# Layer-0 output projection from four plain groups to seven products, with its sums on GpSimd, and all weight sums of the last projection in the z stage

## The chip, the cores and the metric

One core of one Trainium2 chip runs the whole two-layer trunk in one launch. The metric is device time in microseconds (us): the median of three runs of the kernel before is 1525.44 us (1524.47 to 1526.9). Profiles are of one execution on the same core; times in them count from the start of its span. Engines are named as the profile names them: PE (TensorE, matmuls), PEld (its weight loads), DVE (VectorE), ACT (ScalarE), POOL (GpSimd) and SP (the queue that issues the DMAs).

## The reference, cut to what matters

The sequence has 1024 positions, the model 1024 columns, everything is float32. Layer 0 projects its input once, runs a chunked gating unit and a pooling mixer beside each other, gates both, concatenates them to 2048 columns and maps them back; layer 1 is latent attention with a gate and an output projection of the same shape.

```
x <- LN(alpha * x + (1 + gate) * sublayer(x * (1 + scale) + shift))     # both layers
even_mixer: a = gmlp(u, LN(v)) * silu(z_a);  b = pool(x_b) * silu(z_b)
            return concatenate([a, b], -1) @ w_out       # (1024 x 2048) @ (2048 x 1024), layer 0
mla_mixer:  return (o * silu(z)) @ w_out                 # the same shape, layer 1
```

The change concerns the line with `concatenate([a, b]) @ w_out`, and the preparation of layer 1's `w_out`.

## The kernel before, in words

**Numbers in two parts.** A float32 product is made of three fp32r matmuls (`mm3`, L107 to L114): high part times high part, high times low, low times high. `split` (L116 to L121) makes the parts: the high part is a rounding copy on ScalarE (L120), the low part the difference, on VectorE or GpSimd (L121). A tile of 128x1024 (two blocks of 128 rows by 512) is the usual unit; 46 slots of that size (`T`) are shared by all stages, so a load waits until a slot is free.

**Layer 0 in front of the projection.** The input projections run step by step; the u, v, z_a steps are in a seven-product (Strassen-Winograd) form over halves of both operands. The last step is u6 (names u6a to u6d and u6o). Its result is multiplied by the gating unit's output (`gmlp_out`, one half on GpSimd, L829, one on VectorE) and stored to `mix_d` in memory, as are all other blocks of the concatenated activations.

**The output projection of layer 0** (`OutPlain`, object `OP0`) is plain: four groups (two halves of the positions by two halves of the columns), each of 8 chunks q of 256 rows of the contraction, each chunk 4 row tiles x 2 x 3 = 24 matmuls of 128x512 (names y, f0A.., f0W..). Per chunk it loads 512 KB of weights and, in the first and third group, 512 KB of activations, and splits them (ScalarE, VectorE). `evac` applies gate, residual and statistics on VectorE; `norm` and `done0` end a row tile. `to_hT` (names hx, xf, g) turns the rows of the first half for layer 1, in `hook0` at i = 24.

**What the projection carries along** (`hook0`, one call per chunk): the rope tables (`rope_tables`, L1377 to L1400, names ang, kk, RT: some 20 instructions on VectorE of 128x256), three groups of absorbed key weights (`absorb`: each 20 small matmuls, names uk, uq, wab), and two of the four sets of weight sums.

**Weight sums.** The output projection of layer 1 (`OutGated`, object `OP1`) is in the seven-product form. Its weight operands are made ahead: `weight_sums(q)` loads four blocks of `w_out`, multiplies them with the gate on VectorE (L1426), makes four differences on GpSimd (L1431) and stores seven blocks to `wf_d`. Two sets are made in layer 0's projection, two in the z stage.

**The z stage** projects layer 1's gate: eight steps z0 to z7, z0 plain, the others seven products of 12 matmuls each. Every one of these seven steps makes its weight operands with six instructions on GpSimd and five low parts on VectorE, each 128x512, three products ahead of their use. Background work lies in the queue `bg`, from which `pump` takes some after each product.

**What sets the order.** The program is written as one sequence; a scheduler then places the instructions of every engine in a fixed order, in which each engine runs them one after the other, waiting at an instruction until its operands are there. The order of every engine is therefore known, and an instruction that waits holds up all that stand behind it on its engine.

`OutProj`, the parent class of `OutGated`, is in the file before too, and is not used directly: its `prep` takes the engine of each sum and low part from the table `ENG`, by layer and chunk.

Of the kernel before, what the change touches and what calls it, by code (L numbers as in the profile page):

```python
# [17 lines left out]
P = 128  # L18
# [19 lines left out]
ORDER = (1, 6, 5, 7, 4, 3, 2)  # L38


ENG = ({"1B": "VVVV", "1A": "VVVV", "2B": "VVVV", "2A": "GGGG", "6a": "GGGG", "6b": "VVVV",
        "6B": "VVVV", "6c": "VVVG", "6d": "VVGV", "6A": "GGGG", "5B": "VVVV", "5A": "GGGG",
        "7a": "VVVV", "7B": "VVVV", "7b": "VVVV", "7A": "VVVV", "4a": "GGGG", "4B": "VVVV",
        "4A": "VVVV", "3B": "VVVV", "3a": "GGGG", "3A": "VVVV"},
       {"1B": "VVGV", "1A": "VGVG", "2B": "VVVG", "2A": "GGGG", "6a": "GGGG", "6b": "VVVV",
        "6B": "VVVV", "6c": "VVVG", "6d": "VVVV", "6A": "GGGG", "5B": "VVVV", "5A": "GGGG",
        "7a": "VGVG", "7B": "VVVV", "7b": "VVGG", "7A": "GGGG", "4a": "GGVG", "4B": "GVVV",
        "4A": "GGGV", "3B": "VVVV", "3a": "GGGG", "3A": "VVGV"})

NORM = ("MDMDMDDD", "ADADADAD")  # L50

# [29 lines left out]
def trunk_kernel(ctx, tc, x, c, positions, ada_w, ada_b, ln_g, ln_b, e_w_in, gmlp_norm_g,  # L81
# [12 lines left out]
    def T(shape, dt, name):  # L94
        return tp.tile(shape, dt, tag="T", name=name)

    def S2(shape, dt, name):
        return s2.tile(shape, dt, tag="s2", name=name)
# [4 lines left out]
    def B1(shape, name):  # L103
        return pp.tile(shape, F32, tag="b1", name=name)
# [248 lines left out]
    bg = deque()  # L353
# [10 lines left out]
    def mm_nt(HF, W):  # L364

        wf, nkk = W.out, W.nkk

        def mm(ps, fa, fb, start, u):
            for kk in range(4):
                w, h = wf[fa, kk // nkk], HF[fb, kk]  # L370
                mm3(ps, w[:, 0, kk % nkk, :], w[:, 1, kk % nkk, :], h[:, 0, :], h[:, 1, :],
                    start and kk == 0, kk == 3, not start)
        return mm
# [214 lines left out]
    def absorb(g, dma=None):  # L588
        dma = dma or (lambda out, in_: SY.dma_start(out=out, in_=in_))
        uk = S2([P, GH, P], F32, f"uk{g}")  # L590
        uq = [S2([P, GH, NOPE], F32, f"uq{g}{rt}") for rt in range(2)]
        ukT = [None]

        def load():
            dma(out=uk, in_=mla_w_uk[0, :, g * GH:(g + 1) * GH, :])
            for rt in range(2):
                dma(out=uq[rt], in_=mla_w_uq[0, rt * P:(rt + 1) * P, g * GH:(g + 1) * GH, 0:NOPE])

        def turned(src, nm, eng):
            ps = B1([P, GH, P], nm + "p")  # L600
            for h in range(GH):
                PE.transpose(ps[:, h, :], src[:, h, :], ident)
            t = S2([P, GH, P], F32, nm + "T")
            eng(out=t, in_=ps)
            return t

        uqT = [None] * 2

        def keys():
            ukT[0] = turned(uk, f"uk{g}", V.tensor_copy)  # L610

        def query(rt):
            uqT[rt] = turned(uq[rt], f"uq{g}{rt}", A.copy)

        def product(rt):
            wp = B1([P, GH, P], f"wab{g}{rt}")
            for h in range(GH):
                PE.matmul(wp[:, h, :], lhsT=uqT[rt][:, h, :], rhs=ukT[0][:, h, :], start=True, stop=True)
            wab = S2([P, GH * P], F32, f"wabs{g}{rt}")
            V.tensor_scalar(out=wab, in0=wp.rearrange("p h d -> p (h d)"), scalar1=gq[:, rt:rt + 1],  # L620
                            scalar2=None, op0=ALU.mult)
            SY.dma_start(out=wab_d[g, :, rt, :], in_=wab)

        return [load, lambda: (keys(), query(0)), lambda: (product(0), query(1)), lambda: product(1)]
# [12 lines left out]
    n = 0  # L637
# [258 lines left out]
    class OutProj:  # L896
# [45 lines left out]
        def prep(self, p, q):  # L942
# [4 lines left out]
            def eng(x_):  # L947
                return G if ENG[self.l][x_][q] == "G" else V

# [392 lines left out]
    def to_hT(th, Z):  # L1342
        for kk in range(4):
            xt = T([P, 2, 512], F32, f"xf{th}{kk}")
            xf[th, kk] = xt
            for j in range(2):
                k = kk + 4 * j
                ps = B1([P, 512], f"hx{th}{k}")
                for tt in range(4):
                    t = th * 4 + tt  # L1350
                    PE.transpose(ps[:, tt * P:(tt + 1) * P],
                                 Z[k // 4, t // 2][:, t % 2, (k % 4) * P:(k % 4 + 1) * P], ident)
                if XF[th][k] == "A":
                    A.activation(out=xt[:, j, :], in_=ps, func=AF.Identity,
                                 bias=fold[:, 1, k:k + 1], scale=fold[:, 0, k:k + 1])
                else:
                    V.tensor_scalar(out=xt[:, j, :], in0=ps, scalar1=fold[:, 0, k:k + 1],
                                    scalar2=fold[:, 1, k:k + 1], op0=ALU.mult, op1=ALU.add)
                H1.new(form_key(k, th), xt[:, j, :], G if XL[th][k] == "G" else V, f"g{k}_{th}")
# [46 lines left out]
    def weight_sums(q):  # L1406


        r = {}
        IJ = [(i, j) for i in range(2) for j in range(2)]  # L1410

        def load():
            if not gate1:
                g1 = T([P, D], F32, "gate1")
                SY.dma_start(out=g1, in_=gate_d[1].partition_broadcast(P))
                gate1.append(g1)
            for i, j in IJ:
                t = r[i, j] = T([P, 2, 512], F32, f"ws{q}{i}{j}")
                k0 = i * 1024 + q * 256
                SY.dma_start(out=t, in_=o_w_out[0, k0:k0 + 256, j * 512:(j + 1) * 512]  # L1420
                             .rearrange("(k p) c -> p k c", p=P))

        def gated(i, j, n):
            t = r[i, j]
            g1 = gate1[0][:, j * 512:(j + 1) * 512].unsqueeze(1).to_broadcast([P, 2, 512])
            V.tensor_tensor(out=t, in0=t, in1=g1, op=ALU.mult)  # L1426
            if n:
                SY.dma_start(out=wf_d[n - 1, q], in_=t)

        def made(n, to, a, b):  # L1430
            G.tensor_tensor(out=r[to], in0=r[a], in1=r[b], op=ALU.subtract)  # L1431
            SY.dma_start(out=wf_d[n - 1, q], in_=r[to])

        return [load, lambda: None,
                lambda: (gated(0, 0, 1), gated(0, 1, 0)), lambda: (gated(1, 1, 3), gated(1, 0, 2)),
                lambda: made(5, (0, 1), (0, 1), (0, 0)), lambda: made(6, (1, 1), (1, 1), (0, 1)),
                lambda: made(7, (0, 0), (1, 1), (0, 0)), lambda: made(4, (1, 0), (1, 0), (1, 1))]

    later_groups = []
    later_sums = []  # L1440

    def hook0(i):
        if i == 6:
            rope_tables()
        if i % 8 in (1, 2, 3, 4) and i < 24:
            if i % 8 == 1:
                later_groups.extend(absorb(1 + i // 8))
            later_groups.pop(0)()
        if i < 24:
            if i % 12 == 2:  # L1450
                later_sums.extend(weight_sums(i // 12))
            if later_sums:
                later_sums.pop(0)()
        if i == 24:
            to_hT(0, Zs)

    def mix_unit(t, th, q):
        m = 2 * q
        SY.dma_start(out=t, in_=mix_d[m:m + 2, :, th * 512:(th + 1) * 512].rearrange("m d t -> d m t"))

    OP0 = OutPlain(0, e_w_out[0], mix_unit, x[0], done0, (0, 1), (4, 5, 6, 7, 0, 1, 2, 3),
                   lambda n, nm: [B1([P, 512], nm + str(u)) for u in range(4)], hook0)

    def early0(p):
        if p == 1:
            OP0.load_to(0)
        if p in (3, 4):
            OP0.prep_to(p - 3)
        if p == 5:
            OP0.load_to(3)  # L1470
        if p == 6:
            OP0.gate()

# [14 lines left out]
    for s, (stp, post) in enumerate(plan):  # L1488
        nm = stp.nm
# [31 lines left out]

    OP0.run()

# [225 lines left out]

    for m in range(8):  # L1750
        o = [T([P, 2, 512], F32, f"zo{m}{i}") for i in range(2)]
        if m in (1, 4):
            bg += weight_sums(2 + m // 4)
        if m == 0:
            plain(l1, 0, H1, lambda i, j, ps: A.activation(out=o[i][:, j, :], in_=ps, func=AF.Silu))
        else:
            strassen(l1, m, mm_nt(H1, zsteps[m]), lambda u, i, j: o[i][:, j, :], 1, f"z{m}", 3,
                     early1 if m == 7 else None)
        for i in range(2):
            if m:  # L1760
                A.activation(out=o[i], in_=o[i], func=AF.Silu)
            SY.dma_start(out=z_d[2 * m + i], in_=o[i].rearrange("p a b -> p (a b)"))
# [120 lines left out]
    n = len(items)  # L1883
# [36 lines left out]
    for m in range(n):  # L1920
        g, i, first, last = items[m]
# [67 lines left out]
```

## Time and profile before

| | |
|---|---|
| median of three runs | 1525.44 us |
| profiled execution, whole | 1528.2 us |
| its span | 1526.4 us |
| TensorE busy | 1478.0 us, 97% |
| VectorE / ScalarE / GpSimd busy | 69% / 41% / 43% |
| DMA, mean | 138 GB/s |
| granted TensorE clock, mean | 0.99 |

The stages by the trace: input projections of layer 0 until 505 us, its output projection from 505 to some 700, latents of layer 1 (kvq) until 745, z until some 905, attention until 1350, the last projection until the end. A row of the timeline gives start, duration, engine, line, operation, output and inputs (buffer numbers left out, so that tiles of one name read alike), how many instructions it merges, and, in brackets, how long the engine had been idle and what ended that. Durations include a wait that an instruction meets after it has started, so the same instruction can take longer in one place than in another.

### The profile page before, as it was taken

What the parts mean: (1) busy time and instruction counts of PE and PEld (TensorE: products, weight loads), DVE (VectorE), ACT (ScalarE), POOL (GpSimd) and SP (SyncE); (2) the same over time, 40 slices, a digit from 0 to 9 for tenths busy, and PEclk for the clock granted to TensorE, in tenths of its full rate; (3) what the DMA queues carried; (4) which work ended last, traced back from release to release, by engine and by line L of the source; (5) the groups of instructions that cost most, each with busy time, mean ns of one, the idle gap of its engine ahead of it and who ended that gap; (6) DMA issues with size and microseconds to landing.
All of it is one profiled execution on the core that took longest, in us unless ns stands there. A gap on an engine that the chain in (4) does not pass through costs nothing.

```text
span 1526.4 us, 21181 instructions
## 1 busy us (share of the span) xinstructions
PE 1478.0 (97%) x7875; PEld 1269.7 (83%) x7875; DVE 1047.3 (69%) x1660; ACT 622.8 (41%) x1122; POOL 652.0 (43%) x583
## 2 busy tenths in 40 slices
PE   7999998999999999999999999999999999999997
PEld 5888776998898888888888878898989889878885
DVE  6557859574567596556766446777777777668598
ACT  3433323323323323425433445554544545555351
POOL 0033427376567023115776632454444442234245
PEclk9999999999999999999999999999999999999999
DMA  9725543103202799612375551131231131274532
GB/s 300 193 70 200 200 173 110 57 28 111 83 28 90 277 383 333 232 56 77 111 275 193 193 162 59 56 111 42 70 97 56 56 103 33 94 261 139 179 125 97
DMA packets 130771, 210.47 MB, mean 138 GB/s; under 512 B 11774, under 2 KB 78052, under 8 KB 130668
## 3 DMA queue, kind: packets, MB, share of 16 engines
q1 hardware_dynamic: 130668, 209.12, 40.5%
q8 instruction: 62, 1.02, 0.3%
q14 instruction: 41, 0.34, 0.1%
HBM read 152.46 MB, written 56.63 MB: 137 GB/s over the span
## 4 chain that ended last, share of the span: by engine, by line
PE 79%; DVE 9%; DMA 5%; issue 2%; ACT 2%; SPq 1%; POOL 1%; DVEq 0%; POOLq 0%; ACTq 0%
PE pt L1853 4%; PE y L113 3%; PE y L114 3%; PE y L112 3%; PE sc L1785 2%; PE av L113 2%; PE av L112 2%; PE av L114 2%; PE sc L1787 2%; PE sc L1786 2%; PE sc L1789 2%; PE sc L1788 2%; PE zb L113 2%; PE zb L114 2%; DVE mc L753 1%
## 5 line engine op out<-in xcount | busy, mean ns | idle before, releaser
L1836 POOL TENSOR_SCALAR p<-p,rz 128x1024 f32<-128x1024 f32 (+5 forms) x96 | 82.3, 858 | 175.3 <-DVE rz L1835 157.4
L120 ACT CAST pth<-pt 128x512 fp32r<-128x512 f32 x144 | 82.0, 590 | 79.9 <-PE pt L1853 78.9
L121 DVE TENSOR_TENSOR pth<-pt,pth 128x512 fp32r<-128x512 f32 x144 | 96.1, 687 | 24.6 <-ACT pth L120 23.7
L1832 ACT ACTIVATE p<-sc,nm 128x1024 f32<-128x1024 f32 (+5 forms) x96 | 81.8, 853 | 57.4 <-DVE nm L1824 45.9
L1824 DVE TENSOR_REDUCE nm<-sc 128x1 f32<-128x1024 f32 (+5 forms) x96 | 85.1, 887 | 2.0 <-DVE rz L1835 0.2
L1853 PE MATMUL pt<-ident,p 128*128 128x128 f32 x576 | 84.6, 272 | 0.1
L1853 PEld LDWEIGHTS pt<-ident,p 128*128 128x128 f32 x576 | 69.6, 140 | 11.3 <-DVE ol L121 0.3
L1785 PE MATMUL sc<-kvTh,qlh 128*128 128x512 f32 (+4 forms) x192 | 70.6, 368 | 8.3 <-ACT p L1804 3.2
L1431 POOL TENSOR_TENSOR ws<-ws,ws 128x1024 f32<-128x1024 f32 x16 | 43.4, 2724 | 75.0 <-DVE ws L1426 51.8
L1788 PE MATMUL sc<-KRh,qrT 128*128 128x512 f32 (+4 forms) x192 | 66.7, 348 | 0.0
L1789 PE MATMUL sc<-KRl,qrT 128*128 128x512 f32 (+4 forms) x192 | 66.4, 346 | 0.0
L1787 PE MATMUL sc<-kvTh,qll 128*128 128x512 f32 (+4 forms) x192 | 66.3, 345 | 0.0
L1786 PE MATMUL sc<-kvTl,qlh 128*128 128x512 f32 (+4 forms) x192 | 66.1, 344 | 0.0
L112 PE MATMUL av<-pth,kvh 128*128 128x512 f32 x144 | 61.1, 425 | 1.0 <-ACT pth L120 1.0
L113 PE MATMUL av<-pth,kvh 128*128 128x512 f32 x144 | 60.2, 418 | 0.2 <-DVE pth L121 0.2
L114 PE MATMUL av<-pth,kvl 128*128 128x512 f32 x144 | 56.7, 394 | 0.0
L753 DVE SCALAR_TENSOR_TENSOR mc<-mw,cT,mc 128x1024 f32<-128x1024 f32 x28 | 47.5, 1698 | 9.2 <-DMA mw<-in_ada_w_dram 8.8
L1245 POOL TENSOR_TENSOR r1A<-r1A,r1A 128x1024 f32<-128x1024 f32 x12 | 32.3, 2700 | 44.7 <-DMA r1A<-o_d 34.8
L121 DVE TENSOR_TENSOR ol<-av,oh 128x512 fp32r<-128x512 f32 x32 | 22.0, 687 | 39.7 <-ACT oh L120 39.7
L1785 PEld LDWEIGHTS sc<-kvTh,qlh 128*128 128x128 f32 x192 | 36.5, 190 | 14.6 <-ACT p L1832 5.6
L120 ACT CAST oh<-av 128x512 fp32r<-128x512 f32 x32 | 18.8, 587 | 60.1 <-PE av L114 59.7
L1550 POOL TENSOR_TENSOR qrf<-qrf 128x256 f32<-128x256 f32 x32 | 23.6, 737 | 44.6 <-DVE rz L1835 20.1
(1887 smaller groups left out, 5147.8 us busy)
## 6 DMA issues: line engine op xcount, KB each, us to landing
mw<-in_ada_w_dram SPq DMA_DIRECT2D x32, 512.0 KB
r0W<-in_e_w_out_dram SPq DMA_DIRECT2D x32, 512.0 KB
wf_d<-ws SPq DMA_DIRECT2D x28, 512.0 KB
r1W<-wf_d SPq DMA_DIRECT2D x28, 512.0 KB
ada<-in_ada_w_dram SPq DMA_DIRECT2D x32, 256.0 KB
r0A<-mix_d SPq DMA_DIRECT2D x16, 512.0 KB
ws<-in_o_w_out_dram SPq DMA_DIRECT2D x16, 512.0 KB
z_d<-zo SPq DMA_DIRECT2D x16, 512.0 KB
```

The source lines that it names most:

```text
L112: PE.matmul(ps, lhsT=lh, rhs=rh, start=start, stop=False, skip_group_check=more)
L113: PE.matmul(ps, lhsT=lh, rhs=rl, start=False, stop=False, skip_group_check=more)
L114: PE.matmul(ps, lhsT=ll, rhs=rh, start=False, stop=stop, skip_group_check=more)
L120: A.copy(out=hi, in_=src)
L121: eng.tensor_tensor(out=lo, in0=src, in1=f(hi), op=ALU.subtract)
L1785: PE.matmul(o, lhsT=qh[:, h, qs], rhs=kvTh[:, ks], start=True, stop=False)
L1786: PE.matmul(o, lhsT=qh[:, h, qs], rhs=kvTl[:, ks], start=False, stop=False)
L1787: PE.matmul(o, lhsT=qo[:, h, qs], rhs=kvTh[:, ks], start=False, stop=False)
L1788: PE.matmul(o, lhsT=qt[:, h, :], rhs=KRh[:, ks], start=False, stop=False)
L1789: PE.matmul(o, lhsT=qt[:, h, :], rhs=KRl[:, ks], start=False, stop=True)
L1824: V.tensor_reduce(out=nm, in_=sv, axis=AX.XY, op=ALU.max, negate=True)
L1853: PE.transpose(ps[:, h, :], pl[h][:, j * P:(j + 1) * P], ident)
```

## The change

The object `OP0` becomes an `OutProj`: 28 chunks (7 products of 4), 24 matmuls each, in the order of products 1, 6, 5, 7, 4, 3, 2 (names y0a to y0d, f0A.., f0B.., chunk names by place in that order and q, so f0A12 is the activation operand of the second product, 6, in chunk 2). The operands of products 6, 7, 4 and 3 are sums of blocks: for each q four for product 6, two for 7, one each for 4 and 3, all 128x1024. The new table `ENG` puts every sum on GpSimd (keys in small letters) and every low part on VectorE. Halves are taken in the other order: the second half of the positions first, and the pooling branch's half of the contraction as the first block column.

`hook0` now makes the rope tables at chunk 8 (before: 6) and two groups of key weights in the first eight chunks. The last group of key weights, and all four sets of weight sums, move to the z stage (steps 1, 2, 4 and 5).

```diff
-ENG = ({"1B": "VVVV", "1A": "VVVV", "2B": "VVVV", "2A": "GGGG", "6a": "GGGG", "6b": "VVVV",
...
+ENG = ({k: ("GGGG" if k[1].islower() else "VVVV")
+        for k in ("1B", "1A", "2B", "2A", "6a", "6b", "6B", "6c", "6d", "6A", "5B", "5A", "7a", "7B",
+                  "7b", "7A", "4a", "4B", "4A", "3B", "3a", "3A")},)
...
     later_groups = []
-    later_sums = []
 
     def hook0(i):
-        if i == 6:
+        if i == 8:
             rope_tables()
-        if i % 8 in (1, 2, 3, 4) and i < 24:
-            if i % 8 == 1:
-                later_groups.extend(absorb(1 + i // 8))
+        if i < 8:
+            if i % 4 == 0:
+                later_groups.extend(absorb(1 + i // 4))
             later_groups.pop(0)()
-        if i < 24:
-            if i % 12 == 2:
-                later_sums.extend(weight_sums(i // 12))
-            if later_sums:
-                later_sums.pop(0)()
         if i == 24:
             to_hT(0, Zs)
 
-    def mix_unit(t, th, q):
-        m = 2 * q
+    def mix_unit(t, th, kh, q):
+        m = kh * 8 + 2 * q
         SY.dma_start(out=t, in_=mix_d[m:m + 2, :, th * 512:(th + 1) * 512].rearrange("m d t -> d m t"))
 
-    OP0 = OutPlain(0, e_w_out[0], mix_unit, x[0], done0, (0, 1), (4, 5, 6, 7, 0, 1, 2, 3),
-                   lambda n, nm: [B1([P, 512], nm + str(u)) for u in range(4)], hook0)
+    OP0 = OutProj(0, e_w_out[0], mix_unit, x[0], done0, (1, 0), (1, 0),
+                  lambda x_, nm: [B1([P, 512], nm + str(u)) for u in range(4)], hook0)
 
     def early0(p):
         if p == 1:
-            OP0.load_to(0)
+            OP0.load_to(1)
...
-        if m in (1, 4):
-            bg += weight_sums(2 + m // 4)
+        if m == 1:
+            bg += absorb(3)
+        if m in (1, 2, 4, 5):
+            bg += weight_sums(m - 1 - m // 4)
```

What `OutProj.prep` does for a chunk of product n (unchanged code that layer 0 now runs; `sub` runs on the engine that `ENG` names, `op` splits):

```
elif n == 6:
    sub("6a", "B12", "B12", "B11")
    sub("6b", "B22", "B22", "B12")
    op("B", p, q, r["B22", q], eng("6B"))
    sub("6c", "A21", "A21", "A22", ALU.add)
    sub("6d", "A11", "A21", "A11")
    op("A", p, q, r["A11", q], eng("6A"))
elif n == 5:
    ab(r.pop(("B12", q)), r.pop(("A21", q)))
elif n == 7:
    sub("7a", "B11", "B22", "B11")
    op("B", p, q, r.pop(("B11", q)), eng("7B"))
    r["S3", q] = T([P, 2, 512], F32, f"r{self.l}S3{q}")
    sub("7b", "S3", "A22", "A11")
    op("A", p, q, r.pop(("S3", q)), eng("7A"))
elif n == 4:
    sub("4a", "B22", "B21x", "B22")
```

**GpSimd at the start of the projection, before.** After the two products with the gating unit (u4o, u6o) stand the first weight sums (ws, set 0):

```order
L829 TENSOR_TENSOR u4o0_3935<-u4o0_3935,gA4_3725 128x1024
L829 TENSOR_TENSOR u6o0_4137<-u6o0_4137,gA6_3929 128x1024
L1431 TENSOR_TENSOR ws001_4424<-ws001_4424,ws000_4422 128x1024
L1431 TENSOR_TENSOR ws011_4428<-ws011_4428,ws001_4424 128x1024
L1431 TENSOR_TENSOR ws000_4422<-ws011_4428,ws000_4422 128x1024
L1431 TENSOR_TENSOR ws010_4426<-ws010_4426,ws011_4428 128x1024
```

The same place after the change, from u6o on. A name such as r0A210 is the raw block A21 of chunk q = 0:

```order
L824 TENSOR_TENSOR u6o0_4137<-u6o0_4137,gA6_3929 128x1024
L946 TENSOR_TENSOR r0A210_2_4270<-r0A210_2_4270,r0A220_2_4272 128x1024
L946 TENSOR_TENSOR r0B110_0_4173<-r0B220_2_4268,r0B110_0_4173 128x1024
L946 TENSOR_TENSOR r0B121_2_4274<-r0B121_2_4274,r0B111_1_4177 128x1024
L946 TENSOR_TENSOR r0A110_0_4175<-r0A210_2_4270,r0A110_0_4175 128x1024
L946 TENSOR_TENSOR r0A211_2_4278<-r0A211_2_4278,r0A221_2_4280 128x1024
L946 TENSOR_TENSOR r0B122_3_4282<-r0B122_3_4282,r0B112_1_4179 128x1024
L946 TENSOR_TENSOR r0B221_2_4276<-r0B221_2_4276,r0B121_2_4274 128x1024
L946 TENSOR_TENSOR r0A212_3_4286<-r0A212_3_4286,r0A222_3_4288 128x1024
L946 TENSOR_TENSOR r0B123_3_4290<-r0B123_3_4290,r0B113_1_4181 128x1024
L946 TENSOR_TENSOR r0A111_1_4183<-r0A211_2_4278,r0A111_1_4183 128x1024
L946 TENSOR_TENSOR r0B222_3_4284<-r0B222_3_4284,r0B122_3_4282 128x1024
```

Two sums (6a and 6b of chunk 0) stand ahead of u6o; the twelve after it go on with 6c, 7a, 6a, 6d of several chunks in turn. The last sum of product 6 (6d of chunk 3) is the 18th after u6o, and four of 7b follow.

**VectorE in the same stage, before.** The rope table's steps (ang, kk) lie between low parts of the first and second group (f0A07l, f0W10l), eight of them in a row:

```order
L1377 TENSOR_TENSOR ang_4599<-inv_109,C_97 128x256
L1381 TENSOR_SCALAR kk_4601<-ang_4599 128x256
L121 TENSOR_TENSOR f0A07l_4531<-r0A07_4430,f0A07h_4530 128x1024
L1383 TENSOR_SCALAR kk_4601<-kk_4601 128x256
L121 TENSOR_TENSOR f0W07l_4535<-r0W07_4432,f0W07h_4534 128x1024
L1384 TENSOR_SCALAR kk_4601<-kk_4601 128x256
L1385 TENSOR_SCALAR kk_4601<-kk_4601 128x256
L121 TENSOR_TENSOR f0W10l_4571<-r0W10_4481,f0W10h_4570 128x1024
```

After the change they lie between the low parts of product 6 (f0B12l, f0A12l and f0B13l, chunks 2 and 3), with steps of the first product's result (y002, its residual x002):

```order
L1372 TENSOR_TENSOR ang_4741<-inv_109,C_97 128x256
L116 TENSOR_TENSOR f0B12l_4548<-r0B222_3_4284,f0B12h_4547 128x1024
L1376 TENSOR_SCALAR kk_4743<-ang_4741 128x256
L1010 SCALAR_TENSOR_TENSOR y002_4481<-x002_4531,y002_4481 128x512 x2
L1378 TENSOR_SCALAR kk_4743<-kk_4743 128x256
L1379 TENSOR_SCALAR kk_4743<-kk_4743 128x256
L1380 TENSOR_SCALAR kk_4743<-kk_4743 128x256
L1382 TENSOR_TENSOR kk_4743<-kk_4743 128x256
L1385 SCALAR_TENSOR_TENSOR ang_4741<-kk_4743,ang_4741 128x256 x2
L116 TENSOR_TENSOR f0A12l_4554<-r0A112_1_4185,f0A12h_4553 128x1024
L1385 SCALAR_TENSOR_TENSOR ang_4741<-kk_4743,ang_4741 128x256 x2
L116 TENSOR_TENSOR f0B13l_4604<-r0B223_3_4292,f0B13h_4603 128x1024
```

Nine instructions now stand between the two low parts of chunk 2. From z7 on, the orders of all engines are the same before and after, but for a few places.

## Rows read from the trace of the kernel before

**Rows 1.** Page, busy time and share of each engine, whole span

```profile
PE 1478.0 (97%) x7875; PEld 1269.7 (83%) x7875; DVE 1047.3 (69%) x1660; ACT 622.8 (41%) x1122; POOL 652.0 (43%) x583
```

**Rows 2.** Windows: length, PE, PEld, DVE, ACT, POOL busy, PEclk, DMA share, GB/s

```profile
505.00:560.00 55.00, 55.00 (x258) 45.83 (x257) 45.32 (x48) 20.89 (x24) 13.23 (x5) 1.00 0.95 346
560.00:610.00 50.00, 49.58 (x233) 41.13 (x232) 37.94 (x42) 17.39 (x19) 12.82 (x7) 1.00 0.99 344
```

**Rows 3.** Timeline of PE, start of the projection: start, duration, what

```profile
505.61 0.39 PE L112 MATMUL y<-f0W00h,f0A00h 128*128 128x512 f32 x1
...
510.82 0.39 PE L114 MATMUL y<-f0W00h,f0A00l 128*128 128x512 f32 x1
...
531.03 1.05 PE L618 MATMUL wab<-uk1T,uq10T 128*128 128x128 f32 x8
```

**Rows 4.** Timeline of POOL in the projection, 440 to 720 us

```profile
514.74 2.41 POOL L829 TENSOR_TENSOR u6o<-u6o,gA 128x1024 f32<-128x1024 f32 x1 [17.45 <-DVE u6o L406]
...
549.48 7.50 POOL L1431 TENSOR_TENSOR ws<-ws,ws 128x1024 f32<-128x1024 f32 x3 [9.67 <-DVE ang L1390]
...
596.20 2.39 POOL L1431 TENSOR_TENSOR ws<-ws,ws 128x1024 f32<-128x1024 f32 x1 [4.57 <-DMA wf_d<-ws]
...
665.69 5.05 POOL L121 TENSOR_TENSOR g<-xf,g 128x512 fp32r<-128x512 f32 x4 [45.85 <-ACT g L120]
```

**Rows 5.** Timeline of POOL in the last projection, 1372 to 1387 us

```profile
1373.15 12.43 POOL L1245 TENSOR_TENSOR r1A<-r1A,r1A 128x1024 f32<-128x1024 f32 x4 [4.61 <-DVE f1A03l L121]
```

**Rows 6.** Timeline of DVE in the same stretch

```profile
1373.69 2.96 DVE L121 TENSOR_TENSOR f1B10l<-r1W,f1B10h 128x1024 fp32r<-128x1024 f32 x1
1376.57 3.41 DVE L121 TENSOR_TENSOR f1A10l<-r1A,f1A10h 128x1024 fp32r<-128x1024 f32 x1
1379.90 1.28 DVE L1877 TENSOR_TENSOR zt<-uvp,zt 128x512 f32<-128x512 f32 x2
...
1383.26 3.41 DVE L121 TENSOR_TENSOR f1A11l<-r1A,f1A11h 128x1024 fp32r<-128x1024 f32 x1
```

**Rows 7.** Timeline of DVE, 545 to 561 us

```profile
546.61 5.71 DVE L1390 SCALAR_TENSOR_TENSOR ang<-kk,ang 128x256 f32<-128x256 f32 x8
552.35 2.37 DVE L1391 TENSOR_SCALAR ang<-ang 128x256 f32<-128x256 f32 x1
554.76 2.51 DVE L1396 SCALAR_TENSOR_TENSOR kk<-ang 128x256 f32<-128x256 f32 x1
557.19 0.28 DVE L1394 TENSOR_SCALAR RT<-RT 128x256 f32<-128x256 f32 x1
...
557.59 1.21 DVE L121 TENSOR_TENSOR f0W11l<-r0W,f0W11h 128x1024 fp32r<-128x1024 f32 x1
558.73 0.68 DVE L1162 TENSOR_TENSOR y<-y,gate 128x512 f32<-128x512 f32 x1
559.33 0.28 DVE L1400 COPY RT<-RT 128x256 f32<-128x256 f32 x1
```

**Rows 8.** Timeline of PE after its longest wait in layer 0

```profile
260.95 0.79 PE L113 MATMUL pm<-ph,pw 128*128 128x512 f32 x1 [4.25 <-DVE ph L121]
...
262.82 0.63 PE L112 MATMUL za0a<-hT,za0S 128*128 128x512 f32 x1
263.25 0.63 PE L113 MATMUL za0a<-hT,za0S 128*128 128x512 f32 x1
```

**Rows 9.** Windows behind that wait

```profile
261.00:263.00 2.00, 2.00 (x5) 1.61 (x6) 1.66 (x2) 0.83 (x2) 1.16 (x2) 0.50 0.00 0
...
267.00:269.00 2.00, 2.00 (x11) 1.61 (x10) 1.03 (x2) 1.63 (x3) 0.09 (x1) 1.00 0.04 8
```

**Rows 10.** Window of the z stage with its densest set of weight sums

```profile
785.00:805.00 20.00, 20.00 (x89) 16.55 (x90) 14.47 (x13) 8.92 (x16) 17.67 (x11) 1.00 0.75 257
```

**Rows 11.** Page, costliest groups: sums on POOL in the last projection

```profile
L1245 POOL TENSOR_TENSOR r1A<-r1A,r1A 128x1024 f32<-128x1024 f32 x12 | 32.3, 2700 | 44.7 <-DMA r1A<-o_d 34.8
```

**Rows 12.** Groups by line and form: high parts of 128x1024 on ACT

```profile
L120 ACT CAST wz0h<-wz0r 128x1024 fp32r<-128x1024 f32 x2 | 2.1, 1052 | 0.0
```

## What was predicted before the run

> **What bounds the kernel now.** I read the page's busy shares first, then the window table of the layer-0 output projection, then the timelines of TensorE, GpSimd and VectorE around its start. TensorE is busy 97% of the span [rows 1], and in the two windows after 505 us [rows 2] it is busy 55.00 of 55 and 49.58 of 50 us at a granted clock of 1.00: the projection is a stretch in which TensorE never waits, and GpSimd is idle three quarters of it (13.23 and 12.82 us busy). The timeline of TensorE [rows 3] gives the pace: from 505.61 to 510.82 lie 23 steps of one 128x512 matmul, 0.2265 us each. So a matmul taken out is worth 0.2265 us, as long as its successors find their operands. DMA engines are at 0.95 and 0.99 in those windows without TensorE waiting; the change moves fewer bytes there, and I count no gain for it.
>
> **What goes.** The plain form has 4 groups x 8 chunks x 24 = 768 matmuls, the seven-product form 28 x 24 = 672. 96 x 0.2265 = **21.7 us less**. The third group of the absorbed key weights moves to z with its 20 small matmuls; it costs TensorE the same there and is left out of the sum.
>
> **What comes: the sums, and who needs them.** Each of the four chunks q of product 6 needs four sums of 128x1024 on GpSimd (6a, 6b for the weights, 6c, 6d for the activations), then a high part on ScalarE and a low part on VectorE. In the new order of GpSimd the last one, 6d of q=3, stands 18 sums behind the product u6o, because four sums for product 7 (7a) lie between. u6o starts at 514.74 in the trace, when VectorE is done with it [rows 4]; no sum but the first two can go ahead of it.
>
> What a sum costs depends on VectorE. Alone it takes 2.39 us [rows 4]. Where both engines work out of SBUF, they take turns: between 1373.15 and 1385.58 four sums take 12.43 us, and in the same stretch VectorE's low parts of 128x1024, which take 1.21 elsewhere, take up to 3.41 us, while two products that read PSUM take 1.28 together [rows 5, 6]. 3.41 is 2.39 plus one low part at its pace of 1.14 (1.21 at 557.59, the next instruction at 558.73). It holds for small instructions too: of eight 128x256 steps of the rope table in 5.71 us one stands in a sum, the next two take 2.37 and 2.51 where 0.28 is usual, and the three sums beside them take 7.50 us, 2.50 each [rows 4, 7]. So while GpSimd has a sum ready, VectorE gets one instruction per sum, however small, and GpSimd loses that instruction's time.
>
> The Trainium skill (SBUF — State Buffer, section "SBUF: two separate sides") says that the pair of ports VectorE and GpSimd share is an exclusive lock for a whole instruction, taken by whichever starts first, against VectorE instructions in a two-port mode or with two SBUF inputs. The trace agrees that the loser stands still, and it adds that the waiting engine comes next, which the page does not say. Were there no turns, and GpSimd kept the ports until its queue is dry, f0A02l of product 1 would come only 22 x 2.39 = 52.6 us after 518, near 571; six chunks (32.6) and the small matmuls (5.2) follow it, and product 6 would end near 609, 12 us later than by turns. The 12.43 us of [rows 5] speak against that; the dear case below has room for it.
>
> Now the turns, by the new orders of both engines. Low part f0B02l takes the ports first (514.5 to 515.6), u6o follows, and GpSimd is at 518.0.
> - Chunk 0 of product 6 gets its last operand at 535.6: 6 sums (14.3) and A02l, B03l, A03l, B10l, A10l. TensorE is there at 532.6 (96 steps, 12 of u6, 20 small ones) and loses 2 to 3 us at most.
> - Chunk 1 needs f0A11l. From 518.0 there are 12 sums (28.7), seven low parts (8.0) and four 128x512 products with the gate at 0.60 (2.4): 557.1. The copy of the key weights that the next small matmuls need (uk2T) stands behind f0B11l on VectorE, so TensorE already waits before them, from about 541 to 552.
> - Chunk 2 needs f0A12l. The order puts nine instructions of VectorE between f0B12l and f0A12l, seven of them of the rope table, and GpSimd has 10 sums left (the four of 7b are ready and follow at once). 10 x 2.39 = 23.9, plus the turns of VectorE between them (one low part 1.14, two residual steps 1.2, six rope steps 1.6): GpSimd is dry at 584.9; two rope steps and the low part itself: 586.8.
> - Chunk 3 needs f0A13l, 12 more instructions with GpSimd idle: 593.4. Then 16 matmuls: product 6 ends at 597.0.
>
> Without a wait it would end at 505.6 + 192 x 0.2265 (43.5) + 12 matmuls of the last u step (2.7) + 40 small matmuls of two groups of key weights (5.2, at 1.05 for eight, [rows 3]) = 557.0. So the wait costs **40.0 us**. The loads do not set it: the last one for 6c (q=3) is issued behind a store at about 552 and 6c comes at 566.
>
> **After product 6.** Products 5, 7, 4 and 3 have no sum of their own in the way until 4a and 3a, eight sums of 2.39 us. VectorE needs per product eight low parts (9.1) and some eleven 128x512 steps (6.6): 63 of 4 x 21.7 = 87 us, and 19 us in which it stands behind a sum make 82. Nearly full, so a wait of some us is likely where two sums come together: **4 us** (0 to 12; 12 is five of the eight sums uncovered). Product 2 and the start of kvq have the same chain as today.
>
> **Clock.** A wait of 4.25 us at 256.7 was followed by the clock at 0.50 and a pace of 0.43 a matmul (262.82, 263.25) until 266, some twelve, and at 1.00 again in the window from 267 [rows 8, 9]: 12 x 0.20 = 2.4 us. After the long waits of chunk 1 and 2 the same is due; most of it falls into the next wait. **2 us** (0 to 7, three such starts).
>
> **z.** Two more sets of weight sums lie there: 8 sums, 8 products with the gate. The ports again: a z step (84 matmuls, 19.0 us) has six 128x512 instructions on GpSimd at 1.26 (5.05 for four, [rows 4]) and five low parts at 0.60, 10.6 us; a set has 4 x 2.39 + 4 x 1.14 = 14.1. Seven steps hold 133 us; the ports are taken for 102 now and 131 after. Where the set lies densest today, TensorE is busy 20.00 of 20 [rows 10], so the low end is 0. In z2 to z7, where the order puts all 16 sums, 6 x 10.6 + 56.4 = 120 stands against 114 us: 6 over, and twice that if the queues lose as much in waiting. I take **5 us** (0 to 12).
>
> **Sum.** -21.7 + 40.0 + 4 + 2 + 5 = +29.3 us on the span of 1526.4, so 1555.7. The profiled execution took 1528.2 in all, and the median of the runs is 1525.4, 1.0 below the span; the forecast for the median is **1555 us**.
>
> **Rivals.**
> - GpSimd alone is the bound; no turns. For it: the projection of layer 1 runs sums too and its line shows 2.70 us a sum, not 3.4 [rows 11]. Against: that is a mean over covered and bare ones, and [rows 5] shows the turns. 18 sums from 517.15: 560.2 at 2.39, 566.1 at 2.72; high part 1.05 [rows 12], then a chunk: product 6 ends at 566.7 to 572.6, 9.7 to 15.6 late. With 2 us of clock -10.0 to -4.1: 1515 to 1521, faster. The point from which this decides: a wait under 21.7 us, so fewer than about half of VectorE's turns.
> - No wait at all, the sums done in time: 1525.4 - 21.7 = 1504. For it only that GpSimd is idle in the stage; against it that 18 sums at 2.39 are 43 us from 517 and TensorE wants the last at 551.
> - z and the tail come dearer: the ports full from 745 on, 12 in the tail, 7 of clock, 15 to 20 in z: -21.7 + 40.0 + 12 + 7 + 18 = +55, 1580. For it the 131 of 133; against it that a z step's operands are prepared three products ahead, so that a queue may fall behind for a while.
>
> **How the numbers follow.** The turns as above 0.68 (1538 to 1570 by the bounds of its terms), GpSimd alone 0.13, no wait 0.03, dearer 0.16. The range 1528 to 1578 leaves out the two faster cases and part of the dear one. A measurement of this kernel tells 0.2% (3 us) from no change: faster 0.14 (the two cases less their edge), same 0.03, slower 0.83.
>
> **What would show it.** In the changed kernel's timeline: sums on GpSimd in a row from about 518 to 585; low parts f0A10l to f0B12l and the rope steps at 2.4 us and more; TensorE waiting for f0A12l (line of the low part) some 24 us, for uk2T and f0A11l some 12 together, for f0A13l a few; the end of product 6 near 597; 672 matmuls for y0. The forecast is wrong if rope steps between sums take 0.3 us, if the sums take 2.39 each with low parts at 1.2 beside them, or if TensorE has no wait over 10 us before 600.

## The result, and the profile after

The changed kernel takes **1546.94 us** (median of four runs, 1545.01 to 1547.57), the kernel before 1524.95 on the same chip: ratio 1.0148, 95% interval 1.0135 to 1.0161. It is slower by 22 us; the forecast was 1555. The profiled execution took 1547.57 us, its span is 1545.8, 19.4 more than the span before.

The page's busy times of the changed kernel: instructions of each engine behind the x. TensorE has 96 matmuls fewer in all and is busy 11.5 us less, in a span that is longer (its share fell from 97%) [rows 1].

```profile
PE 1466.5 (95%) x7779; PEld 1255.5 (81%) x7779; DVE 1110.9 (72%) x1692; ACT 636.6 (41%) x1142; POOL 759.5 (49%) x615
```

Where the time went is read from the first matmul of each stage. TensorE's timeline of the kernel before, first matmul of kvq, z0 and attention:

```profile
697.41 0.56 PE L112 MATMUL kvq<-wkh,g 128*128 128x448 f32 x2
743.58 0.39 PE L112 MATMUL wz<-g,wz0h 128*128 128x512 f32 x1
900.08 0.28 PE L112 MATMUL qlp<-q0h,wa 128*128 128x256 f32 x1
```

The changed kernel: first matmul of y, of product 5 (where product 6 has ended), kvq, z0 and attention:

```profile
505.93 0.39 PE L107 MATMUL y0a<-f0B00h,f0A00h 128*128 128x512 f32 x1
...
586.11 0.39 PE L107 MATMUL y0c<-f0B20h,f0A20h 128*128 128x512 f32 x1
...
704.96 0.36 PE L107 MATMUL kvq<-wkh,g 128*128 128x448 f32 x1
...
749.25 0.40 PE L107 MATMUL wz<-g,wz0h 128*128 128x512 f32 x1
...
921.21 0.28 PE L107 MATMUL qlp<-q0h,wa 128*128 128x256 f32 x1
```

| stage | before, us | after, us | difference |
|---|---|---|---|
| up to the first y | 505.61 [rows 3] | 505.93 | +0.3 |
| y, to the first kvq | 191.80 | 199.03 | +7.2 |
| kvq | 46.17 | 44.29 | -1.9 |
| z | 156.50 | 171.96 | +15.5 |
| attention and the rest of the span | 626.3 | 624.6 | -1.7 |

So there are two places: the projection, which should have become 24 us shorter and became 7 longer, and z. Each column is one execution, and the stage before y varies by 2 to 3 us even between versions that differ only in z (first y at 505.93 and 503.85, 505.18 and 502.06), so single us mean little here; 7 and 15 do not come from that.

The windows that answer to [rows 2], in the same columns (length, PE, PEld, DVE, ACT and POOL busy, PEclk, DMA share, GB/s):

```profile
505.00:560.00 55.00, 44.47 (x205) 37.07 (x204) 46.81 (x26) 16.89 (x22) 50.64 (x18) 0.88 0.59 211
560.00:610.00 50.00, 40.62 (x168) 32.75 (x167) 45.03 (x47) 19.19 (x23) 27.81 (x8) 0.90 0.17 54
```

TensorE is busy 85 of 105 us where it was busy 104.6; GpSimd went from 13.2 to 50.6 us in the first window. The DMA engines stand at 0.17 in the second, and the long waits below are for VectorE, so the loads don't set the pace. TensorE's timeline at its two long waits (in brackets, idle time before and what ended it):

```profile
550.23 2.05 PE L613 MATMUL wab<-uk2T,uq20T 128*128 128x128 f32 x8 [9.13 <-DVE uk2T L599]
552.07 1.06 PE L597 MATMUL uq21p<-ident,uq 128*128 128x128 f32 x4
553.80 2.08 PE L613 MATMUL wab<-uk2T,uq21T 128*128 128x128 f32 x8 [0.68 <-ACT uq21T L599]
555.53 0.77 PE L107 MATMUL y0a<-f0B11h,f0A11h 128*128 128x512 f32 x1
...
574.46 0.80 PE L109 MATMUL y0a<-f0B12h,f0A12l 128*128 128x512 f32 x1 [9.25 <-DVE f0A12l L116]
575.05 0.63 PE L107 MATMUL y0a<-f0B12h,f0A12h 128*128 128x512 f32 x1
575.47 0.63 PE L108 MATMUL y0a<-f0B12l,f0A12h 128*128 128x512 f32 x1
```

Both are waits for VectorE, and after each the matmuls come at 0.43 us instead of 0.23, at a granted clock of 0.50 (1.2 of 2.4 GHz); at 1.00 the pace is back. Windows in the columns of [rows 2]:

```profile
550.00:554.00 4.00, 3.10 (x13) 2.73 (x14) 0.83 (x2) 0.84 (x2) 4.00 (x3) 0.50 0.02 7
...
574.50:578.50 4.00, 4.00 (x10) 3.17 (x11) 3.93 (x8) 0.00 (x0) 0.00 (x0) 0.50 0.00 0
580.00:584.00 4.00, 4.00 (x19) 3.30 (x18) 3.64 (x4) 0.35 (x1) 0.00 (x0) 1.00 0.21 79
```

GpSimd's timeline, where [rows 4] had one product and a few weight sums:

```profile
515.06 3.31 POOL L824 TENSOR_TENSOR u6o<-u6o,gA 128x1024 f32<-128x1024 f32 x1 [3.12 <-DVE u6o L401]
518.33 3.36 POOL L946 TENSOR_TENSOR r0A<-r0A,r0A 128x1024 f32<-128x1024 f32 x1
521.65 6.68 POOL L946 TENSOR_TENSOR r0B<-r0B,r0B 128x1024 f32<-128x1024 f32 x2
...
553.96 2.37 POOL L946 TENSOR_TENSOR r0A<-r0A,r0A 128x1024 f32<-128x1024 f32 x1
...
565.47 2.39 POOL L946 TENSOR_TENSOR r0B<-r0B,r0B 128x1024 f32<-128x1024 f32 x1
567.82 2.78 POOL L946 TENSOR_TENSOR r0A<-r0A,r0A 128x1024 f32<-128x1024 f32 x1
591.57 14.82 POOL L946 TENSOR_TENSOR r0S<-r0A,r0A 128x1024 f32<-128x1024 f32 x3 [20.97 <-PE y0c L108]
```

Eighteen sums run without a gap from 518.33 to 570.60, 2.90 us each. Then GpSimd stands still for 20.97 us: the four sums 7b (written to the new tiles r0S) start only when matmuls of product 5 have released a slot. VectorE's timeline, from the stretch in front of the first wait on, in the form of [rows 7]:

```profile
535.68 10.52 DVE L1009 TENSOR_TENSOR y<-y,gate 128x512 f32<-128x512 f32 x4
546.12 3.35 DVE L116 TENSOR_TENSOR f0B11l<-r0B,f0B11h 128x1024 fp32r<-128x1024 f32 x1
549.40 0.68 DVE L599 COPY uk2T<-uk2p 128x512 f32<-128x512 f32 x1
...
554.73 2.68 DVE L116 TENSOR_TENSOR f0A11l<-r0A,f0A11h 128x1024 fp32r<-128x1024 f32 x1 [1.66 <-ACT f0A11h L115]
...
558.00 1.93 DVE L1372 TENSOR_TENSOR ang<-inv,C 128x256 f32<-128x256 f32 x1
559.85 3.42 DVE L116 TENSOR_TENSOR f0B12l<-r0B,f0B12h 128x1024 fp32r<-128x1024 f32 x1
563.19 2.47 DVE L1376 TENSOR_SCALAR kk<-ang 128x256 f32<-128x256 f32 x1
565.59 5.57 DVE L1010 SCALAR_TENSOR_TENSOR y<-x,y 128x512 f32<-128x512 f32 x2
571.08 0.28 DVE L1378 TENSOR_SCALAR kk<-kk 128x256 f32<-128x256 f32 x1
...
573.18 1.22 DVE L116 TENSOR_TENSOR f0A12l<-r0A,f0A12h 128x1024 fp32r<-128x1024 f32 x1
...
580.15 1.22 DVE L116 TENSOR_TENSOR f0A13l<-r0A,f0A13h 128x1024 fp32r<-128x1024 f32 x1
```

Up to 570.6 an instruction of VectorE between SBUF tiles takes a sum with it (2.47 us for a step of 128x256, 5.57 for two of 128x512); right behind, the same kind of step takes 0.28 and a low part 1.22. uk2T, a copy out of PSUM (the memory that TensorE writes its results to), takes 0.68 in the middle of the sums: it does not wait for them.

ScalarE's timeline behind the first wait:

```profile
553.16 0.58 ACT L599 COPY uq21T<-uq21p 128x512 f32<-128x512 f32 x1 [11.44 <-PE uq21p L597]
553.65 1.05 ACT L115 CAST f0A11h<-r0A 128x1024 fp32r<-128x1024 f32 x1
```

In z the longest wait is for the low part wz3S. TensorE's row, then VectorE's and GpSimd's rows in front of it (zo, wz: z's own work; ws: weight sums):

```profile
824.36 0.80 PE L109 MATMUL z3c<-gT,wz3S 128*128 128x512 f32 x1 [5.98 <-DVE wz3S L116]
```

```profile
814.86 6.69 DVE L1421 TENSOR_TENSOR ws<-ws,gate 128x1024 f32<-128x1024 f32 x2
821.47 0.68 DVE L401 TENSOR_TENSOR zo<-z2c,zo 128x512 f32<-128x512 f32 x1
822.07 2.23 DVE L116 TENSOR_TENSOR wz3S<-wz3r,wz3S 128x512 fp32r<-128x512 f32 x1
```

```profile
814.35 9.41 POOL L1426 TENSOR_TENSOR ws<-ws,ws 128x1024 f32<-128x1024 f32 x3
```

Two products of VectorE, of one set of weight sums, take turns with three differences of GpSimd, two of them of the set before; the low part that TensorE needs stands behind them.

### The profile page after: what moved, and what is told of

It is laid out like the page before. It is cut to its first block, busy times and chain, and to the rows that moved or that the text cites. A ratio compares the mean times of both kernels' runs of the same rounds, so it can differ in the third digit from the quotient of the medians.

```text
span 1545.8 us, 21082 instructions
## 1 busy us (share of the span) xinstructions
PE 1466.5 (95%) x7779; PEld 1255.5 (81%) x7779; DVE 1110.9 (72%) x1692; ACT 636.6 (41%) x1142; POOL 759.5 (49%) x615
## 4 chain that ended last, share of the span: by engine, by line
PE 71%; DVE 13%; issue 5%; DMA 4%; POOL 3%; ACT 2%; SPq 1%; DVEq 0%; POOLq 0%; ACTq 0%
PE pt L1844 4%; PE sc L1776 2%; PE av L108 2%; PE av L107 2%; PE av L109 2%; PE sc L1777 2%; PE sc L1778 2%; PE sc L1779 2%; PE sc L1780 2%; PE zb L108 2%; PE zb L109 1%; PE y1a L109 1%; PE y1a L108 1%; PE y1a L107 1%; PE zb L107 1%
## 5 line engine op out<-in xcount | busy, mean ns | idle before, releaser
L1823 ACT ACTIVATE p<-sc,nm 128x1024 f32<-128x1024 f32 (+5 forms) x96 | 81.9, 854 | 57.6 <-DVE nm L1815 43.7
L1240 POOL TENSOR_TENSOR r1A<-r1A,r1A 128x1024 f32<-128x1024 f32 x12 | 34.4, 2870 | 43.5 <-DMA r1A<-o_d 34.9
L946 POOL TENSOR_TENSOR r0B<-r0B,r0B 128x1024 f32<-128x1024 f32 x16 | 46.8, 2936 | 14.6 <-DMA r0B<-in_e_w_out_dram 14.5
```

## The experiments

**Engine of the sums.** All sums of the projection on VectorE:

```diff
-ENG = ({k: ("GGGG" if k[1].islower() else "VVVV")
+ENG = ({k: "VVVV"
```

> All sums of the layer-0 projection on VectorE instead of GpSimd, nothing else changed. Theory (GpSimd and VectorE take turns, so a covered pair of sum and low part costs 2.4 + 1.1 us): without GpSimd in the stage a sum costs VectorE about 1.14 us like a low part; 20 sums, 14 low parts and some 12 us of other steps from 505 make about 51 us, so f0A13l comes near 556 and product 6 ends at 558 to 564 instead of 586.1; f0A12l waits under 5 us; total 1522 (1517 to 1528). Rival (the sums are merely too many, whatever engine does them, and VectorE becomes the bound): product 6 ends near 586 or later, total 1545 to 1560.

Measured: 1526.17 us (ratio to the kernel before 1.0005, 0.9994 to 1.0017), 20.8 under the changed kernel and inside the range. The first y is at 505.18, product 5 starts at 562.76: 57.6 us, where the changed kernel has 80.2. f0A13l ends at 558.85 (forecast 556). VectorE does 32 instructions more in all and is done with product 6 sooner. Its timeline, and the window from 505 us; a sum comes every 1.14 us, like a low part:

```profile
529.95 2.34 DVE L946 TENSOR_TENSOR r0B<-r0B,r0B 128x1024 f32<-128x1024 f32 x2
532.22 2.34 DVE L946 TENSOR_TENSOR r0A<-r0A,r0A 128x1024 f32<-128x1024 f32 x2
...
546.17 1.21 DVE L116 TENSOR_TENSOR f0B12l<-r0B,f0B12h 128x1024 fp32r<-128x1024 f32 x1
547.30 1.21 DVE L116 TENSOR_TENSOR f0A12l<-r0A,f0A12h 128x1024 fp32r<-128x1024 f32 x1
```

```profile
505.00:560.00 55.00, 51.16 (x250) 42.21 (x249) 54.23 (x55) 21.11 (x25) 3.30 (x1) 1.00 0.64 218
```

The number of sums is not the trouble; the engine is. This run alone does not tell a slow GpSimd from one that holds VectorE up; the rows of VectorE beside the sums do (f0B12l 3.42 us above, 1.21 here). The Trainium skill (GPSIMD Engine Reference, section "Performance versus the Vector engine") gives GpSimd twice VectorE's time for a two-input sum of twice this width; 2.39 [rows 4] against 1.14 here is a ratio of 2.1.

**z alone.** The kernel before with the z part of the change and the plain projection, without the third key group and the two sets that it carried:

```diff
-        if i % 8 in (1, 2, 3, 4) and i < 24:
+        if i % 8 in (1, 2, 3, 4) and i < 16:
...
-        if i < 24:
-            if i % 12 == 2:
-                later_sums.extend(weight_sums(i // 12))
-            if later_sums:
-                later_sums.pop(0)()
...
-        if m in (1, 4):
-            bg += weight_sums(2 + m // 4)
+        if m == 1:
+            bg += absorb(3)
+        if m in (1, 2, 4, 5):
+            bg += weight_sums(m - 1 - m // 4)
```

> The kernel before with only the z part of the change: third key group and all four sets of weight sums in z, projection left plain. Theory (z pays by itself for two more sets, 12.9 us in the trace after): the projection keeps its time less 2.6 us of key matmuls, z takes about 172 instead of 156.5 us, total 1535 to 1539. Rival (z waits in the changed kernel because the new projection leaves queues, slots or loads late): 1524 to 1529.

Measured: 1536.89 us, ratio 1.0075 (1.0049 to 1.0101). z takes 740.10 to 911.32, 171.2 us, with the same wait of 6.0 us for wz3S; y takes 187.9. So z pays for its two more sets by itself, whatever the projection does.

**The rope table out of product 6.** `rope_tables` called among the u steps:

```diff
-        if i == 8:
-            rope_tables()
...
+        if p == 0:
+            rope_tables()
         if p == 1:
             OP0.load_to(1)
```

> The changed kernel with the rope table made before the projection (among the u steps), so that no step of 128x256 stands between f0B12l and f0A12l. Theory (each of these steps that stands beside a sum costs VectorE up to 2.4 us): f0A12l comes at 567 to 570 instead of 574.4, product 6 ends at 579 to 582 instead of 586.1, total 1541 to 1543. Rival (the sums alone set the end; the last one is done at 570.6 either way): product 6 ends at 584 to 586, total 1545 to 1547.

Measured: 1543.77 us (ratio 1.0114, 1.0085 to 1.0143). From the first y to product 5: 508.69 to 584.63, 75.9 us instead of 80.2. The stage is 4.2 us shorter, as the theory has it, but the absolute times expected were missed by 3 us and the total by one: y starts later (508.69; 502.06 to 505.93 in the other kernels), for a reason that is not shown, and the end of product 6 at 584.63 lies in the rival's range. Of the total, 3.2 us less than the changed kernel, the runs overlap (1542.13 to 1545.6 against 1545.01 to 1547.57), so it is the length of the stage that speaks for the theory. f0A12l now meets a sum (3.36 us).

**7b among the sums.** The failed part of the forecast, tried by itself: 7b needs no new tile, so that it waits for no slot.

```diff
-                r["S3", q] = T([P, 2, 512], F32, f"r{self.l}S3{q}")
-                sub("7b", "S3", "A22", "A11")
-                op("A", p, q, r.pop(("S3", q)), eng("7A"))
+                sub("7b", "A22", "A22", "A11")
+                op("A", p, q, r["A22", q], eng("7A"))
```

> The changed kernel with the sums 7b written over the block A22 instead of a new tile, so that they need no free slot and stand among the sums of product 6 (product 4 then multiplies another block; the output is not the reference's, the work is the same). Theory (the forecast of 597 for the end of product 6 was too late because the four 7b sums stood still for a slot from 570.6 to 591.6): with 22 sums in a row GpSimd is dry at 581 to 585, f0A12l comes at 581 to 588, product 6 ends at 592 to 597; total 1550 to 1556. Rival (7b has no part in it): product 6 ends within 2 us of 586, total 1545 to 1548.

Measured: 1553.98 us (ratio 1.0186, 1.0163 to 1.0210). GpSimd has 22 sums in a row until 579.9 (a us short of the range), f0A12l ends at 584.3, product 6 at 595.08. The end and the total are those of the forecast (597.0, 1555), the path is not: the scheduler also placed the rope steps further ahead, in front of f0A11l, which ends at 567.0 (forecast 557.1), and TensorE's waits are 9.1 us for uk2T, 10.2 for f0A11l, 4.9 for f0B12l and 3.3 for f0A12l. The rope steps now stand in the middle of the sums; VectorE, then GpSimd, in the same stretch:

```profile
556.71 2.32 DVE L1375 TENSOR_SCALAR kk<-ang 128x256 f32<-128x256 f32 x1
559.07 2.32 DVE L1377 TENSOR_SCALAR kk<-kk 128x256 f32<-128x256 f32 x1
561.42 2.31 DVE L1378 TENSOR_SCALAR kk<-kk 128x256 f32<-128x256 f32 x1
563.66 3.35 DVE L116 TENSOR_TENSOR f0A11l<-r0A,f0A11h 128x1024 fp32r<-128x1024 f32 x1
```

```profile
558.85 2.39 POOL L946 TENSOR_TENSOR r0B<-r0B,r0B 128x1024 f32<-128x1024 f32 x1
561.20 2.39 POOL L946 TENSOR_TENSOR r0A<-r0A,r0A 128x1024 f32<-128x1024 f32 x1
563.55 2.38 POOL L946 TENSOR_TENSOR r0B<-r0B,r0B 128x1024 f32<-128x1024 f32 x1
```

Sum and step alternate: one step that takes 0.28 alone per sum of 2.39, in strict order. The end near 609, for a GpSimd that keeps the ports until its queue is dry, is excluded by these rows: it would have let none of the steps through.

**Differences of the weight sums on VectorE**, in the version with all sums there, and in the changed kernel alone:

```diff
-            G.tensor_tensor(out=r[to], in0=r[a], in1=r[b], op=ALU.subtract)
+            V.tensor_tensor(out=r[to], in0=r[a], in1=r[b], op=ALU.subtract)
```

> All sums of the layer-0 projection on VectorE, and the four differences of each set of weight sums in z on VectorE too (16 instructions that were on GpSimd). Theory (z lost its 12.5 us because VectorE and GpSimd stand still for each other: a set's differences take 2.4 to 3.4 us each there): at 1.14 each 16 x 1.25 = 20 us of turns go, the wait of 6.0 us for wz3S goes with its slow clock, and z takes 158 to 163 us instead of 172; total 1512 to 1519, under the kernel before. Rival (z is late for its loads and stores, or VectorE is full): z stays at 169 to 174, total 1523 to 1529.

> The changed kernel with only the differences of the weight sums moved to VectorE. Theory: as before for z alone, 9 to 14 us less: 1533 to 1538; product 6 stays as it is (80 us from its first y0 matmul to the first of product 5). Rival: no change, 1545 to 1548.

Measured: **1512.14 us** for the first, ratio 0.9923 (0.9907 to 0.9938), 13 us under the kernel before; 1533.75 for the second (1.0060, 1.0046 to 1.0074). z takes 161.6 us (723.88 to 885.51) and 161.7 (746.56 to 908.25) instead of 172.0, and the wait for wz3S is 1.6. The ten us are the same in both, so most of z's loss (10.3 of 12.6 us) came from the differences on GpSimd, and the loads were not late; that the two engines stood still for each other there is read from the rows above (two products in 6.69 us, one alone in 1.21).

**The sums left out.** All sums on VectorE, and all but 7b not computed:

```diff
-                eng(x_).tensor_tensor(out=r[out, q], in0=r[a, q], in1=r[b, q], op=o)
+                if x_ == "7b":
+                    eng(x_).tensor_tensor(out=r[out, q], in0=r[a, q], in1=r[b, q], op=o)
```

> All sums of the layer-0 projection on VectorE, but those of 6, 7a, 4 and 3 left out (products multiply raw blocks; the output is not the reference's, the matmuls are all there). Theory (96 matmuls fewer are worth 21.7 us once nothing holds them up, and the third key group has gone to z with 28 small ones, 2.6 to 3 us): from the first y matmul to the first of kvq 167 to 171 us instead of 191.8; total 1515 to 1520. Rival (something else in the seven-product form costs TensorE time, such as evacuations or banks): 174 us or more.

First matmul of y and of kvq:

```profile
503.52 0.39 PE L107 MATMUL y0a<-f0B00h,f0A00h 128*128 128x512 f32 x1
...
670.97 0.36 PE L107 MATMUL kvq<-wkh,g 128*128 128x448 f32 x1
```

Measured: y takes **167.45 us**, 24.35 less than the 191.80 before; the 96 matmuls (21.7) and the key group that left (2.8: 28 small matmuls, groups of 8, 12 and 8 in 0.79, 1.24 and 0.80 us) make 24.5. 1514.73 us in all (0.9935, 0.9913 to 0.9957), with z as long as in the changed kernel. The full gain is there once nothing holds TensorE up; with all sums on VectorE (y 178.0 us) 10.6 us of it are still lost.

**The 7a sums later.** In the best version, product 6 has four 7a sums among its own on VectorE. Written to new tiles, they find no slot before product 5:

```diff
+                r["S4", q] = T([P, 2, 512], F32, f"r{self.l}S4{q}")
-                sub("7a", "B11", "B22", "B11")
-                op("B", p, q, r.pop(("B11", q)), eng("7B"))
+                sub("7a", "S4", "B22", "B11")
+                r.pop(("B11", q))
+                op("B", p, q, r.pop(("S4", q)), eng("7B"))
```

> The version with all sums and weight sums on VectorE, and each 7a sum written to a new tile, for which no slot is free until product 5 runs, so that the four stand behind product 6 on VectorE instead of among its sums. Theory (product 6 is now bound by VectorE at 1.14 us an instruction): three or four instructions of 1.14 us go from in front of f0A13l, product 6 ends 53 to 55 us after its first matmul of y instead of 57.6, and VectorE has room for them before product 7; total 1507 to 1511. Rival (the 7a sums are only late elsewhere, product 7 waits for them): 1512 to 1517.

Measured: 1517.02 us (0.9936, 0.9917 to 0.9956), no gain; the total is at the upper edge of the rival's range. Product 6 takes 54.6 us as expected, but y as a whole 180.2 instead of 178.0: product 7 now waits 1.3 and 1.2 us for f0A32h and f0A33h, as sum, high part and low part of a chunk come one after the other there. So the wait moved with the load, as the rival said.

## Why the forecast was right, and where it was not

The direction, the place and the mechanism (turns of the two engines) were right, and the total, 1555 against 1547, is 8 too high. That it is not further off is in part luck: the wait in product 6 came 14.3 us shorter than forecast, and z 7.6 longer. One of the forecast's own signs of being wrong is met: TensorE has no wait over 10 us before 600, the longest are 9.25 and 9.13. The other two are not: the rope step between the sums took 2.47, and the sums took 2.90 beside low parts of up to 3.42. Its own times against the trace of the changed kernel:

| step | forecast | measured |
|---|---|---|
| GpSimd at the sums | 518.0 | 518.33 |
| f0A10l done | 535.6 | 535.1, TensorE waits 0.7 |
| TensorE's wait for uk2T | 541 to 552 | 541.1 to 550.2 |
| f0A11l done | 557.1 | 557.4 |
| GpSimd dry | 584.9 | 570.6 |
| f0A12l done | 586.8 | 574.4 |
| f0A13l done | 593.4 | 581.4 |
| product 6 ends | 597.0 | 586.1 |

Up to the first wait the alternation of the two engines, one instruction each, gave the times within half a us. The wait ended 2 us sooner than forecast, and f0A11l agrees by another path than the forecast's: its operand was summed by 548.4, the high part f0A11h then stood on ScalarE behind uq21T, which waited for TensorE, and the low part came after that. **The step that failed** is the sentence "GpSimd has 10 sums left (the four of 7b are ready and follow at once)". Their inputs were ready, their destination was not: each 7b writes a new tile, and no slot was free until product 5 [the row at 591.57 above]. With six sums left instead of ten, the rope steps behind 571 met no sum. The kernel without that wait (7b over A22) has GpSimd dry 9.3 us later, about four sums of 2.39, and product 6 ends at 595.08.

The terms of the sum:

| term | forecast | measured |
|---|---|---|
| 96 matmuls | -21.7 | -21.5 (24.35 less the key group, from the run with the sums left out) |
| product 6, wait | 40.0 | 25.7 |
| clock behind it | 2 | 2.6 |
| after product 6 | 4 | 3.3 |
| z | 5 | 12.6 |
| not in the sum: stage before y, kvq, attention | 0 | -3.3 |

Product 6 takes 80.2 us from the first y; less 43.5, 2.7 and two key groups at 2.83 that is 28.3 late. The last long wait ends at 574.46 with 40 matmuls to go, 9.1 us at full pace, and takes 11.65: 2.6 us are the clock, 25.7 the wait (of which TensorE stood idle 19.8 us; the rest is mostly the slow pace behind the first wait). The slow clock behind the first wait (550 to 559, about 4 us lost) disappeared in the second wait, as the forecast had argued: f0A12l would not have come sooner. After product 6 the trace has waits of 1.70, 0.88 and 0.53 us for f0A41l, f0B42l and f0A42l, in the stretch of the sums 4a and 3a as said (f0A41l takes 2.82 beside one); that the sums make all of it is not shown.

Smaller slips changed little. 2.39 plus 1.14 is 3.53, not the 3.41 of [rows 6]. A group of key weights has 28 small matmuls, not the 20 stated ahead of the forecast, so two take 5.7 us and not 5.2. The 2.72 of the first rival is 2.70 in [rows 11].

**z** came out just over its upper bound of 12. The balance of the ports (131 of 133 us) was the right thing to count, but an average over seven steps hides where the instructions lie: at 814 to 824 the end of one set meets the start of the next, and the operand that TensorE needs stands behind both. 8.7 us of waits (5.98, 0.68, 0.35, 0.27, 1.40) and 2.2 of slow clock behind the longest make 10.9 of the 12.6.

Of the rivals, GpSimd alone as the bound is excluded: its 18 sums would have ended at 566 at the latest, not 570.6, product 6 would have been 10 to 16 us late, not 28, and VectorE's instructions beside the sums would not have taken 2.3 to 3.4 us. That the tail would be dear fell too (3.3 us after product 6, where that rival had 12).

## What to carry to other kernels

Where both work between SBUF tiles, count an instruction of GpSimd beside a busy VectorE as time of both: here a covered pair cost the sum of their times (18 sums of 2.39 took 2.90 each with what VectorE put between them), and a step of 0.28 on VectorE cost a whole sum. An idle GpSimd is then no place for such work while VectorE is on the path; here VectorE does it at less than half the price, and 32 sums and 16 differences moved there turn a loss of 22 us into a gain of 13. And before counting work as "ready and next", look at where it writes: a missing destination slot delays it as surely as a missing input.

## What the runs showed that was not expected

A slot that is not free can help: 7b's wait of 20.97 us kept four sums out of product 6; without it, and with the other order of the rope steps that the scheduler chose, the kernel is 7 us slower (1554.0 against 1546.9). The two were not separated.

The busy share misled. In the window from 505 to 560 VectorE shows 46.8 us busy with 26 instructions in the changed kernel, and 54.2 with 55 in the version where it does the sums too: about half of the former was standing in a started instruction (an estimate: at the durations seen without sums beside them, 0.4 to 1.2 us, the 26 take some 22 us).

Versions that differ only behind y still differ in front of it: 505.18 and 502.06 us to the first y matmul with all sums on VectorE, 505.93 and 503.85 with the sums on GpSimd. So stages are compared by their own length.
